# Convolution projection of a hybrid block: four groups of 1024 columns with the tokens on the result's partitions, in place of eight groups of 512 with the features there

## The chip, the cores and the metric

The kernel runs on one core of one Trainium2 chip. The metric is the device time of one execution in microseconds; of several runs the median is taken. A core has TensorE (PE: matmuls into PSUM), VectorE (DVE), ScalarE (ACT), GpSimd (POOL) and SyncE (SP, which issues most loads). Each engine works through its own queue in the order in which the program put it there, and engines wait for each other by semaphores.

## What is computed

One layer: the normalised input `h` (512 tokens, 2048 features) goes through one wide input projection, whose columns feed three branches. The change touches the first, a gated convolution of 1024 channels.

```python
proj = h @ w_in[l]
(c_gate, b_gate, u, conv_z, c_q, c_kv, k_rope_raw, mla_z,
 mem_q, mem_z, g_conv, g_mla, g_mem) = jnp.split(proj, split_at, axis=-1)
conv_y = b_gate * causal_depthwise_conv(c_gate * u, conv_w[l])
o_conv = (conv_y * jax.nn.silu(conv_z)) @ w_conv_out[l]
...
merged = (jax.nn.sigmoid(g_conv) * o_conv + jax.nn.sigmoid(g_mla) * o_mla
          + jax.nn.sigmoid(g_mem) * o_mem)
x = x + merged @ w_o[l]
```

The convolution has three taps over time (the token and the two before it), one set for each channel. `c_gate`, `b_gate`, `u` and `conv_z` have 1024 columns each, so 4096 columns of `w_in` belong to it.

## The kernel before

All is float32, and TensorE gets it in two parts, `hi` (the value as TensorE's fast float32 form holds it) and `lo` (what is left). A product is three matmuls, hi by hi, hi by lo and lo by hi (`mm3`, lines 153 to 155). Weights are split on the way: ACT writes `whi` (line 122), then DVE writes `wlo = raw - whi` (line 124). The pairs `whi`, `wlo` have three buffers, used in turn. Raw weights come in pieces of 128x1024 (512 KB) loaded by SP into ten buffers: four of `wpool` and six of `psw` (`take_raw`, `raws_free`).

The stages of the input projection use a scheme with seven block products in place of eight, on two by two blocks (`PRODUCTS`: P1, P7, P5, P6, P2, P4, P3). For it sums of weight blocks are made on DVE before they are split (`pre`), sums of activation blocks once (`x_forms`: `f` tiles and, by `place_t1`, the T1 blocks), and the seven results are put together from PSUM banks by DVE and ACT (`u`, `v`, `r`).

There are two forms of such a group. In `block_group` the weights are stationary and 256 tokens move: features lie on the result's partitions. A group has 512 columns, 14 chunks of 24 matmuls, 8 raw pieces loaded in pairs (line 943), and four PSUM banks of one tag. The convolution (`conv_group`, eight groups), `mla_z` (four) and the convolution's gate (four) use it. In `block_group_t` the activations are stationary and 512 weight columns move: tokens lie on the result's partitions. A group has 1024 columns, 28 chunks of 12 matmuls, 16 raw pieces loaded one by one (line 1054), and eight banks, four of each tag. The gates of the other two branches, the MLA output projection and the last projection use it.

A planner (`Chunk`, `drive`) writes the queues of PE, DVE, ACT and POOL. At every chunk it puts down, in this order: what is due by a hook (`at`), the weight sums of chunks up to three ahead (`pre`, `first`), the splits of chunks up to two ahead (`prep`, `lead`), what `phases` holds (matmuls of its own, such as transposes), pieces of other work as far as a budget of DVE time goes (`todo`, each with a cost and perhaps a chunk by which it must stand, `by`; then `spare`), and then the chunk's matmuls. A load is entered with `when_raw`: where no raw buffer is free it is put down again at the next chunk.

```python
def hook():
    if len(raws_free if kind is None else [k for k in raws_free if k == kind]) < n:
        when_raw(now[0] + 1, n, kind, fn)
    else:
        fn()
at[c].append(hook)
```

Of the convolution, `conv_group` takes a group's results with features on partitions and all 512 tokens in a row: it multiplies `c_gate` by `u` (line 1431), takes the taps (ACT line 1436, DVE line 1438 twice), multiplies by `b_gate` and by silu of `conv_z` (line 1443), and stores 128 channels to `adram` for the output projection, which comes much later. The stage ahead of it is `mem_z` (`plain_group`), the one behind it `mla_z`.

Of the kernel before, what the change touches and what calls it, by code (L numbers as in the profile page):

```python
# [94 lines left out]
def body(ctx, tc, a, out):  # L95
# [21 lines left out]
    def bank(tag):  # L117
        return psum.tile([P, 512], F32, tag=tag, name=tag)
# [95 lines left out]
    def g(col):  # L214
        return gains[:, col:col + 1]
# [824 lines left out]
                    k.done = results(name)  # L1040
        return first

    def block_group_t(src, tokens, results, early=6, opening=(), again=False):

        first = len(plan)
        w, kinds, bk, sc = {}, {}, {}, {}

        def load(i):
# [39 lines left out]

        for name, ch in order:
            bn, xn = {n: (b, x) for n, b, x in PRODUCTS}[name]
            hold = {}

            def pre(name=name, ch=ch, hold=hold):
                w00, w01 = w[ch], w[4 + ch]
                if name == "P7":
                    hold["s"] = psw.tile([P, KC, 512], F32, tag="s3", name="s3", bufs=2).rearrange("p k n -> p (k n)")
                    vec.tensor_tensor(out=hold["s"], in0=w00, in1=w01, op=ALU.subtract)  # L1100
                else:
                    hold["s"] = o = w01 if name == "P5" else w00
                    i0, i1, op = {"P5": lambda: (w01, w[8 + ch], ALU.add), "P6": lambda: (w01, w00, ALU.subtract),
                                  "P3": lambda: (w[12 + ch], w00, ALU.subtract)}[name]()
                    vec.tensor_tensor(out=o, in0=i0, in1=i1, op=op)  # L1105

            def prep(name=name, ch=ch, hold=hold):
                src_ = hold["s"] if "s" in hold else w[{"P1": 0, "P4": 8, "P2": 12}[name] + ch]
                hi, lo = parts_tile()
                split(src_, hi, lo)  # L1110
                raws_free.extend(kinds[i] for i in {"P5": (4 + ch,), "P4": (8 + ch,), "P3": (ch, 12 + ch)}.get(name, ()))
                hold["w"] = tuple(t.rearrange("p (k n) -> p k n", k=KC) for t in (hi, lo))

            def mm(name=name, ch=ch, bn=bn, xn=xn, hold=hold):
                opens = bn not in bk
                if not bk:

                    t, o = next_tag()
                    bk["tags"] = dict(zip("XWYZ", (t, t, o, o)))
                    if not again:  # L1120
                        tags[0] += 1
                if opens:
                    bk[bn] = [bank(bk["tags"][bn]) for _ in range(2)]
                last = name in ("P2", "P3", "P4", "P6")
                for tb in range(2):
                    cols = slice(tb * P, (tb + 1) * P)
# [19 lines left out]
    def f_tile(p):  # L1146
        return pf.tile([P, 2, 3, HS], F32R, name=f"f{p}")
# [205 lines left out]
    plan[first].lead = 1  # L1353
    take_memz(first, banks_z1, 1)

    tx = [None] * 8
    t1s = {}

    def x_forms(p):

# [14 lines left out]
                    nc.gpsimd.dma_start(out=eo[:, i], in_=hdram[k][:, 1], accum_op=ALU.add)  # L1375

        def sums():
            f = f_tile(p)
            tx[p] = operands(xt[p], xt[p + 8], f)
# [30 lines left out]
            at[CLOSE + 1 + p].append(lambda p=p: spare.extend(  # L1410
                (0.42, lambda q=q: place_t1(q)) for q in range(p - 3, p + 1)))

    for c, n in ((9, 12), (12, 4), (14, 0)):
        at[first + c].append(lambda n=n: flush_spare(n))


    def conv_group(cb):
        keep = {}

        def consume(half, r):  # L1420
            wc = G_CONV + 3 * cb
            if half:
                def silu():
                    keep["bz"] = r()
                    act.activation(r()[:, 1], r()[:, 1], AF.Silu)
                return [(1, 0, silu)]

            def cu():
                used["y"] += 1
                keep["cu"] = pres.tile([P, S], F32, tag="y", name="cu", bufs=4)  # L1430
                vec.tensor_tensor(out=keep["cu"], in0=r()[:, 0], in1=r()[:, 1], op=ALU.mult)

            def tap(n):
                cv, u = r()[:, 0, 2 - n:], keep["cu"][:, :S - 2 + n]
                if n == 2:
                    act.activation(cv, u, AF.Copy, scale=g(wc + 2))
                else:
                    vec.scalar_tensor_tensor(out=cv, in0=u, scalar=g(wc + n), in1=cv, op0=ALU.mult, op1=ALU.add)
                if n == 0:
                    freed("y")  # L1440

            def times(nb):
                vec.tensor_tensor(out=r()[:, 0], in0=r()[:, 0], in1=keep["bz"][:, nb], op=ALU.mult)
            return [(0, 0.69, cu), (1, 0, lambda: tap(2)), (1, 0.75, lambda: tap(1)), (1, 0.75, lambda: tap(0)),
                    (2, 0.69, lambda: times(0)), (2, 0.69, lambda: times(1)),
                    (4, 0, lambda: nc.scalar.dma_start(adram[8 + cb], r()[:, 0]))]
        return consume

    def mlaz_group(grp, first):
        ys = {}  # L1450
# [64 lines left out]
            return out_ + [(2, 0, lambda tb=tb: store(tb)) for tb in range(2)]  # L1515
        return results

    AFTER_PLAIN = (-3, -2, -1, 0)
    for cb in range(8):
        if cb == 0:  # L1520
            block_group(a["w_conv"][cb], tx, conv_group(cb), AFTER_PLAIN, halves=True)
        else:
            block_group(a["w_conv"][cb], tx, conv_group(cb))
    for grp in range(4):
        block_group(a["w_mlaz"][grp], tx, mlaz_group(grp, len(plan)))
    for grp in range(4):
# [308 lines left out]
def layout(inp):  # L1835
# [29 lines left out]
    a["w_conv"] = np.stack([two_by_two(w_in, [(c * 1024 + b * P, P) for c in (0, 2, 1, 3)]) for b in range(8)])  # L1865
# [22 lines left out]
```

## Time and profile before

| | us |
|---|---|
| median of 3 runs | 2144.67 |
| lowest and highest | 2143.73, 2145.27 |
| the profiled execution, its own time | 2144.14 |
| its span, first to last instruction | 2142.4 |
| PE busy | 2117.1 (99%) |
| DVE busy | 1565.1 (73%) |
| ACT busy | 1031.4 (48%) |
| mean granted TensorE clock | 0.999 |

The profile is of one execution. Busy time counts a moment once, however many matmuls overlap in it. A row of a timeline gives start, duration, engine, source line, tiles (out<-in) and, in brackets, how long the engine had been idle and who released it. Line numbers are those of the printed kernel.

### The profile page before, as it was taken

How to read it: one execution, taken by the hardware profiler on the slowest of the kernel's cores; microseconds unless marked ns; L12 is line 12 of the kernel's file. 1: busy time of each engine (PE TensorE's matmuls, PEld its weight loads, DVE VectorE, ACT ScalarE, POOL GpSimd, SP SyncE). 2: the span in 40 equal slices, each digit the busy share in tenths (PEclk: the TensorE clock that was granted, in tenths of full speed). 3: DMA queues.
4: the chain of work that ended last, by engine and by line, in shares of the span. 5: the costliest groups of instructions: out<-in, count | busy, mean ns of one | idle time of the engine just before them, and what ended most of it. 6: DMA issues, size and time to landing. Idle time of an engine off the chain costs nothing.

```text
span 2142.4 us, 31861 instructions
## 1 busy us (share of the span) xinstructions
PE 2117.1 (99%) x12504; PEld 1889.9 (88%) x12504; DVE 1565.1 (73%) x2230; ACT 1031.4 (48%) x1559; POOL 146.4 (7%) x193
## 2 busy tenths in 40 slices
PE   8999999999999999999999999999999999999999
PEld 6898888888888999999999999888888888887887
DVE  7853877773346877877877767777776788857987
ACT  7633676764334444444444444445445434434433
POOL 0000312120001000000000000000000001121000
PEclk9999999999999999999999999999999999999999
DMA  8572212144239324223345334344335755486452
GB/s 306 194 241 87 77 55 69 65 153 162 89 108 295 121 103 137 94 101 137 109 177 177 128 109 158 104 142 167 118 118 178 275 186 206 150 286 202 149 196 89
DMA packets 110119, 322.35 MB, mean 150 GB/s; under 512 B 13200, under 2 KB 13456, under 8 KB 109968
## 3 DMA queue, kind: packets, MB, share of 16 engines
q1 hardware_dynamic: 78480, 253.89, 34.3%
q10 hardware_dynamic: 21600, 38.63, 4.8%
q0 software_dynamic: 9888, 27.79, 4.7%
q8 instruction: 98, 1.61, 0.3%
q14 instruction: 53, 0.43, 0.1%
HBM read 269.41 MB, written 48.23 MB: 148 GB/s over the span
## 4 chain that ended last, share of the span: by engine, by line
PE 92%; DVE 3%; ACT 2%; DMA 1%; issue 1%; POOL 0%; ACTq 0%; DVEq 0%; POOLq 0%
PE acc L154 16%; PE acc L153 16%; PE acc L155 16%; PE aux L154 13%; PE aux L155 13%; PE aux L153 13%; PE aux L657 1%; PE aux L204 1%; DVE wlo L124 0%; ACT whi L146 0%; PE aux L637 0%; PE aux L638 0%; PE aux L639 0%; DMA mraw<-in_memT 0%; PE aux L641 0%
## 5 line engine op out<-in xcount | busy, mean ns | idle before, releaser
L122 ACT ACTIVATE whi<-raw 128x1024 fp32r<-128x1024 f32 x440 | 466.1, 1060 | 661.6 <-PE aux L154 159.1
L124 DVE TENSOR_TENSOR wlo<-raw,whi 128x1024 fp32r<-128x1024 f32 x440 | 538.6, 1225 | 336.1 <-ACT whi L122 329.0
L147 DVE TENSOR_TENSOR wlo<-raw,whi 128x1024 fp32r<-128x1024 f32 (+3 forms) x97 | 106.1, 1094 | 90.1 <-ACT whi L146 88.5
L146 ACT ACTIVATE whi<-raw 128x1024 fp32r<-128x1024 f32 (+3 forms) x97 | 92.8, 957 | 114.6 <-PE acc L154 41.6
L153 PE MATMUL acc<-whi,blk 128*128 128x512 f32 (+1 forms) x352 | 132.5, 380 | 2.1 <-DVE qt L582 1.4
L155 PE MATMUL acc<-whi,blk 128*128 128x512 f32 (+1 forms) x352 | 131.4, 374 | 0.0
L154 PE MATMUL acc<-wlo,blk 128*128 128x512 f32 (+1 forms) x352 | 131.1, 373 | 0.0
L1105 DVE TENSOR_TENSOR raw<-raw 128x1024 f32<-128x1024 f32 x96 | 116.9, 1218 | 0.0
L1015 DVE TENSOR_TENSOR raw<-raw 128x1024 f32<-128x1024 f32 x96 | 116.9, 1218 | 0.0
L122 ACT ACTIVATE whi<-s 128x1024 fp32r<-128x1024 f32 x64 | 67.9, 1061 | 93.6 <-PE aux L154 21.0
L155 PE MATMUL acc<-f,wlo 128*128 128x256 f32 x384 | 108.7, 283 | 0.0
L153 PE MATMUL acc<-f,whi 128*128 128x256 f32 x384 | 108.7, 283 | 0.0
L154 PE MATMUL acc<-f,whi 128*128 128x256 f32 x384 | 108.7, 283 | 0.0
L153 PE MATMUL aux<-f,whi 128*128 128x256 f32 x384 | 108.7, 283 | 0.0
L154 PE MATMUL aux<-f,whi 128*128 128x256 f32 x384 | 108.7, 283 | 0.0
L155 PE MATMUL aux<-f,wlo 128*128 128x256 f32 x384 | 108.7, 283 | 0.0
L1200 POOL DMA_DIRECT2D y<-gdram x48 | 26.4, 550 | 1198.2 <-DMA gdram<-gy 953.9
L154 PE MATMUL acc<-blk,whi 128*128 128x256 f32 (+1 forms) x320 | 97.5, 305 | 0.6 <-DVE blk L124 0.6
L153 PE MATMUL acc<-blk,whi 128*128 128x256 f32 (+1 forms) x320 | 97.8, 306 | 0.0
L153 PE MATMUL acc<-hU,whi 128*128 128x256 f32 (+1 forms) x320 | 97.5, 305 | 0.0
L153 PE MATMUL aux<-hU,whi 128*128 128x256 f32 (+1 forms) x320 | 97.5, 305 | 0.0
L153 PE MATMUL aux<-blk,whi 128*128 128x256 f32 (+1 forms) x320 | 97.4, 305 | 0.0
(458 smaller groups left out, 6239.4 us busy)
## 6 DMA issues: line engine op xcount, KB each, us to landing
raw<-in_w_conv SPq DMA_DIRECT2D x64, 512.0 KB, 4.3
raw<-in_w_mlaz SPq DMA_DIRECT2D x32, 512.0 KB, 5.0
raw<-in_w_gconv SPq DMA_DIRECT2D x32, 512.0 KB, 4.3
raw<-in_w_gmem SPq DMA_DIRECT2D x32, 512.0 KB, 3.3
raw<-in_w_gmla SPq DMA_DIRECT2D x32, 512.0 KB, 3.3
raw<-in_w_mla_out SPq DMA_DIRECT2D x32, 512.0 KB, 3.9
raw<-in_w_o SPq DMA_DIRECT2D x32, 512.0 KB, 3.7
raw<-in_w_mem_kv SPq DMA_DIRECT2D x31, 512.0 KB, 4.1
```

The costliest lines, as they stand in the source:

```text
L122: act.activation(hi, src, AF.Copy, scale=1.0 if g is None else g)
L124: vec.tensor_tensor(out=lo, in0=src, in1=r32(hi), op=ALU.subtract)
L146: act.activation(hi[:, cols], raw[:, cols], AF.Copy)
L147: vec.tensor_tensor(out=lo[:, cols], in0=raw[:, cols], in1=r32(hi[:, cols]), op=ALU.subtract)
L153: nc.tensor.matmul(o, lhsT=s[0], rhs=m[0], start=start, stop=False, skip_group_check=shared)
L154: nc.tensor.matmul(o, lhsT=s[0], rhs=m[1], start=False, stop=False, skip_group_check=shared)
L155: nc.tensor.matmul(o, lhsT=s[1], rhs=m[0], start=False, stop=stop, skip_group_check=shared)
L204: nc.tensor.transpose(out=b[:, i * P:(i + 1) * P], in_=s, identity=ident)
L657: nc.tensor.transpose(out=b[:, i * P:(i + 1) * P], in_=ps[i][:, j * P:(j + 1) * P], identity=ident)
L1015: vec.tensor_tensor(out=o, in0=i0, in1=i1, op=op)
L1105: vec.tensor_tensor(out=o, in0=i0, in1=i1, op=op)
L1200: eng.dma_start(t, src)
```

## The change

The convolution's projection becomes four groups of `block_group_t` (`conv_rows` in place of `conv_group`): a group holds 256 columns each of `c_gate`, `u`, `b_gate` and `conv_z`. The result of name "n t" (two by two blocks) now has tokens on the partitions: "0t" holds `c_gate` and `u` side by side, "1t" `b_gate` and `conv_z`. Their products are made there (`mul`, 256 wide), and then turned by 16 transposes of 128x128 for a group (`turn`, put down ahead of the fourth chunk of what follows), so that the taps run along the tokens as before. The group's order is that of `opening`: all chunks of P1 and P7, then those of P5 and P6, then P4, then P2 and P3. `paired` puts X and Y into banks of one tag and W and Z into the other, and turns the tags once for a group. The `f` tiles are now taken at one time (`x_operands`), and the last steps of the activations' forms are flushed one chunk later. The weights of the convolution are laid out in another order outside the kernel.

```diff
-    def block_group_t(src, tokens, results, early=6, opening=(), again=False):
+    def block_group_t(src, tokens, results, early=6, opening=(), again=False, paired=False):
...
             def mm(name=name, ch=ch, bn=bn, xn=xn, hold=hold):
-                opens = bn not in bk
+                opens = name in ("P1", "P7", "P5", "P6") and ch == 0
                 if not bk:
 
                     t, o = next_tag()
-                    bk["tags"] = dict(zip("XWYZ", (t, t, o, o)))
-                    if not again:
+                    bk["tags"] = dict(zip("XYWZ" if paired else "XWYZ", (t, t, o, o)))
+                    if not (again or paired):
                         tags[0] += 1
-                if opens:
-                    bk[bn] = [bank(bk["tags"][bn]) for _ in range(2)]
+                if opens and bn not in bk:
+                    for b in "WZ" if paired and bn == "Z" else bn:
+                        bk[b] = [bank(bk["tags"][b]) for _ in range(2)]
...
+    def x_operands():
+        for p in range(8):
+            fx[p] = f_tile(p)
+            tx[p] = operands(xt[p], xt[p + 8], fx[p])
+    at[CLOSE].append(x_operands)
...
-    for c, n in ((9, 12), (12, 4), (14, 0)):
+    for c, n in ((10, 12), (13, 4), (15, 0)):
         at[first + c].append(lambda n=n: flush_spare(n))
...
+        def turn():
+            t = keep["kind"]()
+            bs = [transpose4([s[:, f * P:(f + 1) * P] for s in b], t) for b in (cu, bz) for f in range(2)]
...
+                def tap(n, f=f, hold=hold, wc=wc):
+                    if n == 2:
+                        used["y"] += 1
+                        hold["t"] = pres.tile([P, S], F32, tag="y", name="cv", bufs=4)
+                        act.activation(hold["t"], bs[f], AF.Copy, scale=g(wc + 2))
+                        return
+                    cv = hold["t"][:, 2 - n:]
+                    vec.scalar_tensor_tensor(out=cv, in0=bs[f][:, :S - 2 + n], scalar=g(wc + n), in1=cv,
+                                             op0=ALU.mult, op1=ALU.add)
+
+                def times(f=f, hold=hold):
+                    vec.tensor_tensor(out=hold["t"], in0=hold["t"], in1=bs[2 + f], op=ALU.mult)
+                    later(1, 0, lambda: stored(f, hold["t"]))
...
+                later(0, 0, piece(lambda tap=tap: tap(2), **by))
+                later(0, 0.75, piece(lambda tap=tap: tap(1), **by))
+                later(0, 0.75, piece(lambda tap=tap: tap(0), **by))
+                later(0, 0.69, piece(times, **by))
+        phases[first + 31].append(turn)
...
-    for cb in range(8):
-        if cb == 0:
-            block_group(a["w_conv"][cb], tx, conv_group(cb), AFTER_PLAIN, halves=True)
-        else:
-            block_group(a["w_conv"][cb], tx, conv_group(cb))
+    for cb in range(4):
+        opening = [(n, ch) for n in ("P1", "P7") for ch in range(4)] if cb == 0 else \
+            [("P" + n, int(ch)) for n, ch in zip("11717177", "01021323")]
+        opening += [(n, ch) for ch in range(4) for n in ("P5", "P6")]
+        block_group_t(a["w_conv"][cb], tx, conv_rows(cb), 5 if cb == 0 else 6, opening, paired=True)
```

The new lines that the text below names are, in the changed kernel: L1057 the load of a piece, L1103 and L1108 the weight sums, L1435 `mul`, L1456 and L1476 the sums of results, L1472 the product taken from PSUM, L1504 the taps and L1508 the product by the gate. Names in the order that follows are tiles (out<-in); in brackets stand the semaphores that an instruction waits for, by the engine or the DMA queue that raises them.

PE, at the border between two groups of before (features on partitions, `hU` and `blk` moving):

```order
L153 MATMUL acc<-hU_6105,whi 128x256
L154 MATMUL acc<-hU_6105,whi 128x256
L155 MATMUL acc<-hU_6105,wlo 128x256
L153 MATMUL aux<-blk,whi 128x256 [waits Activation_49]
L154 MATMUL aux<-blk,whi 128x256
L155 MATMUL aux<-blk,wlo 128x256 [waits DVE_49]
```

PE, after the first three chunks of the second group of the changed kernel:

```order
L155 MATMUL aux<-whi,f_7176 128x512
L204 MATMUL acc<-ident,cu 128x128
L204 MATMUL acc<-ident,cu 128x128 [waits DVE_49]
L204 MATMUL acc<-ident,u_7691 128x128 [waits DVE_49] x2
L204 MATMUL acc<-ident,cu 128x128 x2
L204 MATMUL acc<-ident,u_7691 128x128 x2
L204 MATMUL acc<-ident,v_7790 128x128 [waits PE_49]
L204 MATMUL acc<-ident,v_7790 128x128 x3
```

The matmuls have gone from 256 to 512 columns, and the transposes of the group before, which wait for DVE, stand among those of the next.

DVE, in a group of before, from the product of `c_gate` and `u` to the first sum of the next results:

```order
L1431 TENSOR_TENSOR cu<-r_8390 128x512
L1015 TENSOR_TENSOR raw<-raw 128x1024
L124 TENSOR_TENSOR wlo<-raw,whi 128x1024 [waits DVE_49,PE_49,Activation_49]
L1015 TENSOR_TENSOR raw<-raw 128x1024
L124 TENSOR_TENSOR wlo<-raw,whi 128x1024 [waits PE_49,Activation_49]
L1438 SCALAR_TENSOR_TENSOR r_8390<-cu,gains,r_8390 128x511
L1438 SCALAR_TENSOR_TENSOR r_8390<-cu,gains,r_8390 128x510 [waits DVE_49]
L124 TENSOR_TENSOR wlo<-raw,whi 128x1024 [waits PE_49,Activation_49]
L1443 TENSOR_TENSOR r_8390<-r_8390,r_8330 128x512 [waits DVE_49] x2
L124 TENSOR_TENSOR wlo<-raw,whi 128x1024 [waits DMAHW6_49,PE_49,Activation_49]
```

DVE, in the second group of the changed kernel, from the first tap to the `wlo` of chunk 11 (the chunks P5 and P6 of the first two quarters):

```order
L1504 SCALAR_TENSOR_TENSOR cv<-acc,gains,cv 128x511
L1504 SCALAR_TENSOR_TENSOR cv<-acc,gains,cv 128x510 [waits DVE_49]
L1508 TENSOR_TENSOR cv<-cv,acc 128x512 [waits DVE_49]
L1108 TENSOR_TENSOR raw<-raw 128x1024
L124 TENSOR_TENSOR wlo<-raw,whi 128x1024 [waits Activation_49]
L1108 TENSOR_TENSOR raw<-raw 128x1024 [waits DMAHW0_49]
L124 TENSOR_TENSOR wlo<-raw,whi 128x1024 [waits Activation_49]
L1108 TENSOR_TENSOR raw<-raw 128x1024 [waits DVE_49]
L124 TENSOR_TENSOR wlo<-raw,whi 128x1024 [waits Activation_49]
L1108 TENSOR_TENSOR raw<-raw 128x1024 [waits DMAHW4_49]
L124 TENSOR_TENSOR wlo<-raw,whi 128x1024 [waits Activation_49]
```

The same taps of two blocks stand in one piece ahead of the first P5's split (the first block's three are just ahead of these rows), and a sum that waits for a load (DMAHW4) stands ahead of a split that needs none.

SP, the loads of the second group of the changed kernel from its piece 8 on:

```order
L1057 DMA raw<-in_w_conv 128x1024 [waits DMAHW7_49,DVE_49]
L1057 DMA raw<-in_w_conv 128x1024 [waits DMAHW0_49]
L1057 DMA raw<-in_w_conv 128x1024 [waits DMAHW1_49,DVE_49]
L1057 DMA raw<-in_w_conv 128x1024 [waits DMAHW4_49,DVE_49]
L1057 DMA raw<-in_w_conv 128x1024 [waits DMAHW5_49,DVE_49]
```

A load raises the semaphore of the queue that it names first: these are the pieces 8, 9, 11, 10 and 12 in this order, and the third and fourth wait for DVE to have read a buffer.

## Rows read from the trace of the kernel before

**Rows 1.** The page: its head, part 1 (busy time and share of the span of each engine) and the first line of part 4 (the chain of work that ended last, by engine).

```profile
span 2142.4 us, 31861 instructions
...
PE 2117.1 (99%) x12504; PEld 1889.9 (88%) x12504; DVE 1565.1 (73%) x2230; ACT 1031.4 (48%) x1559; POOL 146.4 (7%) x193
...
PE 92%; DVE 3%; ACT 2%; DMA 1%; issue 1%; POOL 0%; ACTq 0%; DVEq 0%; POOLq 0%
```

**Rows 2.** Windows: the first convolution group, the second, and a group of `block_group_t` (a gate); columns are the stretch, its length, busy time and instructions of PE, PE's weight loads, DVE, ACT and POOL, granted clock, DMA share and GB/s.

```profile
694.29:735.45 41.16, 40.57 (x337) 40.36 (x336) 33.18 (x40) 20.69 (x28) 0.00 (x0) 1.00 0.40 142
735.45:775.77 40.32, 40.32 (x338) 40.32 (x337) 32.20 (x33) 17.55 (x19) 0.00 (x0) 1.00 0.32 112
...
1340.00:1416.10 76.10, 76.10 (x339) 63.06 (x338) 57.32 (x53) 35.94 (x40) 0.00 (x0) 1.00 0.40 139
```

**Rows 3.** Timeline of PE: the first matmul of the convolution, the one gap in its first group, and the first matmul of the stage behind it.

```profile
694.29 0.28 PE L153 MATMUL acc<-blk,whi 128*128 128x256 f32 x1
...
711.93 0.29 PE L153 MATMUL acc<-blk,whi 128*128 128x256 f32 x1
712.82 0.38 PE L154 MATMUL acc<-blk,whi 128*128 128x256 f32 x1 [0.59 <-DVE blk L124]
...
1017.70 0.28 PE L153 MATMUL acc<-blk,whi 128*128 128x256 f32 x1
```

**Rows 4.** Timeline of PE in the stage `mem_z`, 512 moving: two matmuls with 143 others between them, back to back.

```profile
639.89 0.39 PE L153 MATMUL acc<-hU,whi 128*128 128x512 f32 x1
...
672.53 0.39 PE L153 MATMUL aux<-hU,whi 128*128 128x512 f32 x1
```

**Rows 5.** Timeline of PE at a block of 16 transposes in the convolution's output projection.

```profile
1902.67 0.39 PE L155 MATMUL acc<-act,wlo 128*128 128x512 f32 x1
1902.90 1.91 PE L1701 MATMUL aux<-ident,f 128*128 128x128 f32 x16
1904.56 0.48 PE L153 MATMUL acc<-act,whi 128*128 128x512 f32 x1
1904.88 0.40 PE L154 MATMUL acc<-act,whi 128*128 128x512 f32 x1
```

**Rows 6.** Groups of DVE instructions by line and shape (count, busy us, mean ns of one), in the convolution's groups two to eight and, the last, around its first group.

```profile
L124 DVE TENSOR_TENSOR wlo<-raw,whi 128x1024 fp32r<-128x1024 f32 x84 | 102.7, 1223 | 52.4 <-ACT whi L122 51.5
L1015 DVE TENSOR_TENSOR raw<-raw 128x1024 f32<-128x1024 f32 x42 | 51.1, 1218 | 0.0
...
L1443 DVE TENSOR_TENSOR r<-r,r 128x512 f32<-128x512 f32 x14 | 9.6, 689 | 0.2
...
L1154 DVE TENSOR_TENSOR raw<-eo 128x256 f32<-128x256 f32 x7 | 2.9, 418 | 0.0
```

**Rows 7.** Timeline of DVE in the third convolution group around the taps: a weight sum, a split, the two taps, a split and two products.

```profile
787.47 1.22 DVE L1015 TENSOR_TENSOR raw<-raw 128x1024 f32<-128x1024 f32 x1
788.61 1.22 DVE L124 TENSOR_TENSOR wlo<-raw,whi 128x1024 fp32r<-128x1024 f32 x1
789.74 1.53 DVE L1438 SCALAR_TENSOR_TENSOR r<-cu,gains,r 128x511 f32<-128x511 f32 x2
791.40 1.23 DVE L124 TENSOR_TENSOR wlo<-raw,whi 128x1024 fp32r<-128x1024 f32 x1
792.55 1.41 DVE L1443 TENSOR_TENSOR r<-r,r 128x512 f32<-128x512 f32 x2
794.28 1.23 DVE L124 TENSOR_TENSOR wlo<-raw,whi 128x1024 fp32r<-128x1024 f32 x1 [0.32 <-ACT whi L122]
```

**Rows 8.** Timelines of PE, ACT and DVE in a group of `block_group_t`: the last matmul of a chunk, the `whi` that waits for it, and the `wlo` behind that.

```profile
1418.94 0.39 PE L155 MATMUL aux<-whi,blk 128*128 128x512 f32 x1
...
1419.42 1.06 ACT L122 ACTIVATE whi<-raw 128x1024 fp32r<-128x1024 f32 x1 [1.66 <-PE aux L155]
...
1420.51 1.23 DVE L124 TENSOR_TENSOR wlo<-raw,whi 128x1024 fp32r<-128x1024 f32 x1 [0.30 <-ACT whi L122]
```

**Rows 9.** Timelines of DVE and of SP's queue: a `wlo` that gives back its raw buffer, and the load that goes into it.

```profile
1406.86 1.23 DVE L124 TENSOR_TENSOR wlo<-raw,whi 128x1024 fp32r<-128x1024 f32 x1 [0.36 <-ACT whi L122]
...
1408.12 0.33 SPq L1054 DMA_DIRECT2D raw<-in_w_gmem  x1
```

**Rows 10.** DMA issues, each with its count, KB and median us from issue to landing: of 1393 to 1394 (a lone load), of 1394 to 1395 (a load issued 1.4 us behind that one), of 1418.9 to 1420.2 (a load with two stores), and of the whole span for the convolution's weights.

```profile
raw<-in_w_gmem SPq DMA_DIRECT2D x1, 512.0 KB, 3.2
...
raw<-in_w_gmem SPq DMA_DIRECT2D x1, 512.0 KB, 4.1
...
raw<-in_w_gmem SPq DMA_DIRECT2D x1, 512.0 KB, 4.2
gdram<-gy ACTq DMA_DIRECT2D x2, 256.0 KB, 4.6
...
raw<-in_w_conv SPq DMA_DIRECT2D x64, 512.0 KB, 4.3
```

**Rows 11.** Timeline of PE around the one fall of the granted clock in mid-kernel.

```profile
1962.96 0.71 PE L1701 MATMUL acc<-ident,f 128*128 128x128 f32 x5
1966.24 1.26 PE L1701 MATMUL acc<-ident,f 128*128 128x128 f32 x8 [2.57 <-ACT hU L1715]
1967.16 0.78 PE L153 MATMUL aux<-act,whi 128*128 128x512 f32 x1
...
1970.29 0.52 PE L154 MATMUL aux<-act,whi 128*128 128x512 f32 x1
1970.65 0.39 PE L155 MATMUL aux<-act,wlo 128*128 128x512 f32 x1
...
1967.00:1971.00 4.00, 4.00 (x14) 3.25 (x13) 3.87 (x8) 2.59 (x5) 1.09 (x2) 0.57 0.59 197
```

More of the change, by code (lines that the diff above doesn't have):

```diff
@@ L1041, in block_group @@
         return first
-    def block_group_t(src, tokens, results, early=6, opening=(), again=False):
+    def block_group_t(src, tokens, results, early=6, opening=(), again=False, paired=False):
         first = len(plan)
         w, kinds, bk, sc = {}, {}, {}, {}
+        if paired:
+            results.keep["kind"] = lambda: bk["tags"]["X"]
         def load(i):
@@ L1354, in body @@
     take_memz(first, banks_z1, 1)
-    tx = [None] * 8
+    tx, fx = [None] * 8, [None] * 8
     t1s = {}
+    def x_operands():
[3 more added lines that the diff above has]
+    at[CLOSE].append(x_operands)
     def x_forms(p):
@@ L1377, in sums @@
         def sums():
-            f = f_tile(p)
-            tx[p] = operands(xt[p], xt[p + 8], f)
+            f = fx[p]
             if p % 4 == 0:
@@ L1411, in body @@
                 (0.42, lambda q=q: place_t1(q)) for q in range(p - 3, p + 1)))
-    for c, n in ((9, 12), (12, 4), (14, 0)):
+    for c, n in ((10, 12), (13, 4), (15, 0)):
         at[first + c].append(lambda n=n: flush_spare(n))
[L1417 to L1436, printed above, removed]
-                else:
-                    vec.scalar_tensor_tensor(out=cv, in0=u, scalar=g(wc + n), in1=cv, op0=ALU.mult, op1=ALU.add)
-                if n == 0:
-                    freed("y")
[L1442 to L1447, printed above, removed]
@@ new lines, in conv_rows, with mul, results, silu @@
+    def conv_rows(cb):
+        first = len(plan)
+        cu, bz, keep = [None] * NTB, [None] * NTB, {}
+        hcols, lcols = slice(HS, 2 * HS), slice(0, HS)
+        def mul(o, t):
+            vec.tensor_tensor(out=o, in0=t[:, lcols], in1=t[:, hcols], op=ALU.mult)
+        def results(name, o, i0, i1):
+            out_ = []
+            last = dict(by=first + 30)
+            for tb in range(2):
+                if name == "11":
+                    def silu(tb=tb):
+                        act.activation(o(tb)[:, hcols], o(tb)[:, hcols], AF.Silu)
+                    def gate(tb=tb):
+                        keep[tb] = o(tb)
+                        bz[2 + tb] = o(tb)[:, lcols]
+                        mul(bz[2 + tb], o(tb))
+                    out_ += [(0, 0, piece(silu, **last)), (1, 0.42, piece(gate, **last))]
+                elif name == "10":
+                    hold = {}
+                    def sums(tb=tb, hold=hold):
+                        used["y"] += 1
+                        hold["t"] = pres.tile([P, S], F32, tag="y", name="gy", bufs=4)
+                        vec.tensor_tensor(out=hold["t"], in0=i0(tb), in1=i1(tb), op=ALU.add)
+                        act.activation(hold["t"][:, hcols], hold["t"][:, hcols], AF.Silu)
+                    def gate(tb=tb, hold=hold):
+                        bz[tb] = keep[tb][:, hcols]
+                        mul(bz[tb], hold["t"])
+                        freed("y")
+                    out_ += [(0, 0.69, piece(sums, by=first + 24)), (1, 0.42, piece(gate, **last))]
+                elif name == "00":
+                    def both(tb=tb):
+                        if tb == 0:
+                            used["y"] += 1
+                            keep["cu"] = pres.tile([P, S], F32, tag="y", name="cu", bufs=4)
+                        cu[tb] = keep["cu"][:, tb * HS:(tb + 1) * HS]
+                        act.activation(cu[tb], i0(tb)[:, hcols], AF.Copy)
+                        vec.tensor_tensor(out=cu[tb], in0=i0(tb)[:, lcols], in1=cu[tb], op=ALU.mult)
+                    out_ += [(0, 0.42, piece(both, **last))]
+                else:
+                    def sums(tb=tb):
+                        vec.tensor_tensor(out=o(tb), in0=i0(tb), in1=i1(tb), op=ALU.add)
+                    def both(tb=tb):
+                        cu[2 + tb] = o(tb)[:, lcols]
+                        mul(cu[2 + tb], o(tb))
+                    out_ += [(0, 0.69, piece(sums, by=first + 28)), (0, 0.42, piece(both, **last))]
+            if name == "01":
+                out_.sort(key=lambda t: -t[1])
+            return out_
+        def turn():
+            t = keep["kind"]()
+            bs = [transpose4([s[:, f * P:(f + 1) * P] for s in b], t) for b in (cu, bz) for f in range(2)]
+            freed("y")
+            freed("r0")
+            freed("r1")
+            by = dict(by=first + 33)
+            for f in range(2):
+                hold = {}
+                wc = G_CONV + 3 * (2 * cb + f)
+                def tap(n, f=f, hold=hold, wc=wc):
+                    if n == 2:
+                        used["y"] += 1
+                        hold["t"] = pres.tile([P, S], F32, tag="y", name="cv", bufs=4)
[7 more added lines that the diff above has]
+                    later(1, 0, lambda: stored(f, hold["t"]))
+                def stored(f, t):
+                    nc.scalar.dma_start(adram[8 + 2 * cb + f], t)
+                    freed("y")
+                later(0, 0, piece(lambda tap=tap: tap(2), **by))
[3 more added lines that the diff above has]
+        phases[first + 31].append(turn)
+        results.keep = keep
+        return results
@@ L1516, in gate_rows @@
         return results
-    AFTER_PLAIN = (-3, -2, -1, 0)
-    for cb in range(8):
-        if cb == 0:
-            block_group(a["w_conv"][cb], tx, conv_group(cb), AFTER_PLAIN, halves=True)
-        else:
-            block_group(a["w_conv"][cb], tx, conv_group(cb))
+    for cb in range(4):
[3 more added lines that the diff above has]
+        block_group_t(a["w_conv"][cb], tx, conv_rows(cb), 5 if cb == 0 else 6, opening, paired=True)
     for grp in range(4):
@@ L1864, in layout @@
     a["w_mem_out"] = groups(i["w_mem_out"][0], 0, 2048)
-    a["w_conv"] = np.stack([two_by_two(w_in, [(c * 1024 + b * P, P) for c in (0, 2, 1, 3)]) for b in range(8)])
+    a["w_conv"] = np.stack([two_by_two_t(np.concatenate([w_in[:, c * 1024 + b * HS:c * 1024 + (b + 1) * HS] for c in (0, 2, 1, 3)], axis=1))
+                            for b in range(4)])
     a["w_gconv"] = np.stack([two_by_two(w_in, [(9280 + i * 512, 512)]) for i in range(4)])
```

## The prediction

> **What bounds the kernel now.** Read the page first: TensorE is busy for 99% of a span of 2142.4 us and the chain that ended last is 92% PE, while DVE is at 73% and ACT at 48% [rows 1]. So the time is nearly the sum of matmul pitches (start of one to start of the next), plus the moments when PE waits. The duration in a row of a matmul (0.28 us, 0.39 us) is no price, because matmuls overlap; the pitch has to be taken from two starts far apart.
>
> Next the windows table. A convolution group of before takes 40.32 us on PE, and DVE is busy for 32.2 us of it, ACT for 17.6; the first group takes 41.16 [rows 2]. The stage runs from 694.29 to 1017.70, 323.41 us for 2688 matmuls with 256 moving [rows 3]. One gap is in it: the matmul after 711.93 starts at 712.82 and not 0.12 later, for lack of a `wlo` from DVE [rows 3]. Less that 0.8, the pitch is 322.6 / 2688 = 0.120 us.
>
> **Part 1, the matmuls.** The change does the same seven products with 4 x 336 = 1344 matmuls, 512 moving. Such a matmul stands in the trace already: from 639.89 to 672.53 are 144 of them, 0.2267 us each [rows 4]. 1344 x 0.2267 = 304.7 us, against 323.4: **-18.7 us**. PE is the bound here, so all of it counts. The Trainium skill ("TensorE: Matmul & The Clock Gate", section "Back-to-back issue gap") gives columns / 2.4 plus 2.5 ns for an isolated gap, 109 and 216 ns; by that the trade would give 3.5 us and not 17.9. The rows decide: both pitches are 11 ns longer, and that fixed part is paid half as often.
>
> **Part 2, the transposes.** Each group ends in `turn`: 16 transposes of 128x128 from SBUF. The trace has 16 such in a row: they start at 1902.90, the matmul behind them at 1904.56 and the next at 1904.88; from 1902.67 to 1904.88 is 2.21 us, of which two matmuls are 0.45, so 1.76 for the block [rows 5]. 4 x 1.76 = **+7.0 us**, all on PE. The Trainium skill (same page, "Part 4: PE-mode transpose") gives about 275 ns for one. The rows agree on the duration, not on the cost in a row: 64 x 275 ns would be 17.6 us, where the pitch gives 7.0.
>
> **Part 3, DVE and the waits that it makes.** DVE works in strict order, so I lay its queue end to end with row prices: `wlo` and a weight sum 1.14 us from start to start, a tap 0.83 (the second waits for the first), a 512-wide product 0.6, a 256-wide one 0.33 [rows 6, 7]. A split starts late, not early: ACT may write `whi` only when the buffer used three chunks before is read; it starts 0.25 us after the next chunk's first matmul (1419.42 against 1419.17, which is 1418.94 + 0.23), and DVE's `wlo` starts 1.34 after it [rows 8]. A chunk is 12 x 0.2267 = 2.72 us.
>
> *The turn.* It stands ahead of chunk 3 of the next group, at 3 x 2.72 = 8.16 us. Its last operands (L1435, two products) stand behind the `wlo` of chunk 4, which starts at 5.44 + 1.34 = 6.78; + 1.14 + 0.33 + 0.42 = 8.67. PE wants the fourth transpose at 8.47: 0.2 us, three times, and about twice that in front of the next stage: **+1.0 us**.
>
> *The taps.* Four taps and two products are queued ahead of the `wlo` of chunk 8, the first P5. Counted from the start of chunk 5: 1.34, `wlo` of chunk 7 1.14, taps and products 2 x (1.66 + 0.6) = 4.5, a weight sum 1.13, `wlo` of chunk 8 1.22: 9.33. PE wants it at 8.16 + 0.23 = 8.39: 0.9 us, in three groups: **+2.7 us**. In groups of before two taps stand there and DVE still had idle time left [rows 2, 7].
>
> *The loads.* This is the term that decides. The group now holds 16 raw pieces in 10 buffers. Pieces 0 to 7 stay until P5 and P3, 8 and 9 take the last two; 10 and 11 must wait for buffers that the `wlo` of P5 gives back. `when_raw` puts off a load that finds no buffer by re-entering it behind those due later, so piece 11 goes first although piece 10 is used first (the order shows the two waits the other way round). Piece 10 is then issued only after the `wlo` of chunk 10. The sum for P5 of chunk 12 needs it, and the `wlo` of chunk 11 is queued behind that sum. From the same zero: `wlo` of chunk 8 starts at 8.11; sum, `wlo`, sum take 1.14 + 3 x 1.13 until `wlo` of chunk 10 starts at 12.64, ending at 13.86. A freed buffer's load is issued 0.03 us later (1406.86 + 1.23 = 1408.09, issue 1408.12) [rows 9]. Landing: 3.2 us for a lone load, 4.2 beside two stores issued with it, 4.1 when it follows another by 1.4 us, 4.3 the median of this matrix's loads in pairs [rows 10]. ACT issues the group's two stores at this very place, so I take 4.1: 18.0; sum 1.13, `wlo` 1.22: 20.35. PE wants it at 8.16 + 0.94 + 3 x 2.72 + 0.23 = 17.49. **2.9 us, three times: +8.6** (bounds 2.0 and 3.1 each, for 3.2 and 4.3).
>
> In group 0 no taps stand, but the rest of the activations' forms do. Piece 9 takes the buffer of the T1 scratch, free after the last `blk` split. From PE's first matmul: 1.15, then 7 `wlo` and 6 sums 14.8, four 512-wide gates 2.5, nine 256-wide pieces 3.1, a split 0.6, short waits 0.7: 22.8. Landing behind piece 10's load 4.0, sum 1.13, `wlo` 1.22: 29.2, wanted at 9 x 2.72 + 0.23 = 24.7: **+4.5 us** (3.7 to 4.8).
>
> **Part 4, the clock.** The granted clock fell once in the middle of before: five transposes from 1962.96, 2.57 us idle, eight more, and from 1967.16 matmuls come 0.43 us apart, the 1.2 GHz level, until about 1970.65 [rows 11]. Eight matmuls took 3.5 us and not 1.8: 1.7 us lost. Ahead of it the engine had had 4.2 us of only transposes and idle time. Group 0's wait of 4.5 is longer, so I count **one fall, +1.7**; the 2.9 us waits are between nothing and this, and I count none for them (bound: three, +5.1).
>
> What costs nothing: the bytes loaded are the same; ACT has 22 us free of 40 [rows 2]; the form steps moved one chunk later have P1's and P7's eight chunks ahead of T1's first use; the `adram` stores are read hundreds of us later.
>
> **Sum.** -18.7 + 7.0 + 1.0 + 2.7 + 8.6 + 4.5 + 1.7 = +6.8. The profiled execution took 2144.14 us, its span and 1.7 around it, 0.5 under the median of 2144.67 and within its runs: 2144.1 + 6.8 = **2150.9**, said as 2151.
>
> **Rivals.** *The loads land like lone ones* (3.2 us, rows 10): the waits shrink by 0.8 + 3 x 0.9 = 3.5, and with no fall of the clock the time is 2145.7, no change to be seen. For it: loads are now single. Against: stores and a second load stand beside each of the four. Chance 0.22.
>
> *The loads do not hold DVE at all*, the other side: a buffer free one chunk and a half earlier than I lay it, so that piece 10 lands before DVE comes to its sum (it decides below about 1.2 us from the end of chunk 10's `wlo`, or if piece 10 goes first). Then only the small waits stay: 2144.1 - 18.7 + 7.0 + 1.0 + 2.7 = 2136.1. For it: before shows no PE wait for any load of this matrix. Against: there the loads went in pairs with eight pieces to a group. Chance 0.08.
>
> *All at its worst*: loads of 5.3 us as two crowded ones would give, and a fall of the clock after every wait: 2150.9 + 4.8 + 5.1 = 2160.8. Chance 0.07.
>
> *No gain in a wider matmul*, 512 moving at twice 0.120: 1344 x 0.240 = 322.6, 2168.8. The Trainium skill's gap rule of part 1 leans this way. Rows 4 speak against it. Chance 0.01.
>
> **How the numbers follow.** The forecast has 0.62, from 2149.2 (no fall) to 2156.0 (four). A measurement can tell about 0.2% of this kernel, 4.3 us, from no change, so slower begins at 2149.0: 0.62 + 0.07 + 0.01, less 0.05 for the forecast's own lower edge, 0.65. Same: 0.22 + 0.05 = 0.27. Faster: 0.08. The range takes in the first rival and the falls of the clock, 2145 to 2157, and leaves out the other rivals and the edges.
>
> **What would show it.** Right: conv matmuls 0.227 apart; blocks of 16 transposes of 1.76; in each later group a PE wait of about 3 us for `wlo` in chunk 11, with DVE idle for a DMA ahead of L1108; about 4.5 us in chunk 9 of group 0. Wrong: no DVE wait for `raw<-in_w_conv`, PE without gaps over 1 us, or a stage (first convolution matmul to the first of `mla_z`, transposes included) under 318 us.

## The result and the profile after

The changed kernel takes 2150.91 us (median of 7 runs, 2149.8 to 2154.13), the kernel before 2144.64 (7 runs, 2141.26 to 2145.27): a ratio of 1.0034, 95% interval 1.0023 to 1.0046. It is slower, by little more than a measurement can tell. The profiled execution took 2151.38, its span 2149.6, at a mean granted clock of 0.997.

The page of the changed kernel first, its head, part 1, the two lines of part 4 and one group of part 5.

```profile
span 2149.6 us, 29212 instructions
...
PE 2113.2 (98%) x11224; PEld 1828.5 (85%) x11224; DVE 1566.0 (73%) x2246; ACT 1030.8 (48%) x1567; POOL 146.3 (7%) x193
...
PE 89%; DVE 5%; ACT 3%; DMA 2%; issue 1%; SPq 0%; POOL 0%; ACTq 0%; DVEq 0%; POOLq 0%
PE acc L154 16%; PE acc L153 15%; PE acc L155 15%; PE aux L154 13%; PE aux L155 13%; PE aux L153 13%; DVE wlo L124 1%; DVE raw L1108 1%; PE aux L204 1%; DMA raw<-in_w_conv 1%; PE aux L657 1%; ACT whi L122 0%; DMA raw<-in_w_conv_out 0%; DVE cv L1504 0%; PE aux L637 0%
...
L1108 DVE TENSOR_TENSOR raw<-raw 128x1024 f32<-128x1024 f32 x144 | 175.4, 1218 | 15.0 <-DMA raw<-in_w_conv 15.0
```

Against [rows 1], 1280 matmuls are gone and the busy time of PE fell by only 3.9 us; PE's share of the chain fell from 92% to 89%, and DVE, ACT and DMA took it over. The last line is the new thing: DVE stood idle for 15.0 us ahead of weight sums, for loads of the convolution's weights. The view of waits says who paid (engine, line, waited for, total us, times, longest).

```profile
PE aux L154 <- DVE wlo L124: 8.1, 4, 4.6
...
PE acc L154 <- DVE wlo L124: 5.2, 4, 1.9
```

and, for DVE:

```profile
DVE raw L1108 <- DMA raw<-in_w_conv: 15.0, 4, 4.4
```

Four waits of DVE for a load, one in each group. The timeline of PE shows where they come out: first and last matmul of the stage (the last row belongs to `mla_z`), the gap in chunk 9 of group 0, two matmuls of a quiet stretch, one block of transposes, and chunks 8 and 11 of group 1.

```profile
695.96 0.39 PE L153 MATMUL acc<-whi,blk 128*128 128x512 f32 x1
...
720.60 0.39 PE L153 MATMUL aux<-whi,f 128*128 128x512 f32 x1
725.60 0.80 PE L154 MATMUL aux<-wlo,f 128*128 128x512 f32 x1 [4.61 <-DVE wlo L124]
...
739.71 0.39 PE L155 MATMUL aux<-whi,f 128*128 128x512 f32 x1
...
759.89 0.39 PE L154 MATMUL aux<-wlo,hU 128*128 128x512 f32 x1
...
786.63 0.39 PE L155 MATMUL aux<-whi,f 128*128 128x512 f32 x1
786.87 0.38 PE L204 MATMUL acc<-ident,cu 128*128 128x128 f32 x2
...
788.03 1.04 PE L204 MATMUL acc<-ident,v 128*128 128x128 f32 x8
788.83 0.47 PE L153 MATMUL aux<-whi,blk 128*128 128x512 f32 x1
789.14 0.39 PE L154 MATMUL aux<-wlo,blk 128*128 128x512 f32 x1
...
802.55 0.39 PE L153 MATMUL acc<-whi,blk 128*128 128x512 f32 x1
803.62 0.50 PE L154 MATMUL acc<-wlo,blk 128*128 128x512 f32 x1 [0.68 <-DVE wlo L124]
...
811.69 0.39 PE L153 MATMUL acc<-whi,f 128*128 128x512 f32 x1
814.02 0.67 PE L154 MATMUL acc<-wlo,f 128*128 128x512 f32 x1 [1.94 <-DVE wlo L124]
...
1024.84 0.28 PE L153 MATMUL acc<-blk,whi 128*128 128x256 f32 x1
```

A gap costs its start-to-start distance less one pitch. Group 0 loses 5.00 - 0.23 = 4.77 us, chunk 8 loses 0.84, chunk 11 2.10; groups 2 and 3 read the same way, 0.84 and 0.84, 2.25 and 2.06. From 739.71 to 759.89 are 89 pitches of 0.2267. The stage takes 328.88 us, against 323.41 before [rows 3], and one block of transposes still lies behind it.

The cause of the wait in chunk 11 of group 1 can be read from three timelines (DVE, SP's queue, ACT's queue). They are put in order of time within each engine.

```profile
806.89 1.22 DVE L124 TENSOR_TENSOR wlo<-raw,whi 128x1024 fp32r<-128x1024 f32 x1
811.61 1.23 DVE L1108 TENSOR_TENSOR raw<-raw 128x1024 f32<-128x1024 f32 x1 [3.50 <-DMA raw<-in_w_conv]
812.75 1.22 DVE L124 TENSOR_TENSOR wlo<-raw,whi 128x1024 fp32r<-128x1024 f32 x1
...
808.14 0.33 SPq L1057 DMA_DIRECT2D raw<-in_w_conv  x1
...
807.10 0.81 ACTq L1512 DMA_DIRECT2D adram<-cv  x2
```

The `wlo` of chunk 10 ends at 808.11 and gives back a buffer; 0.03 later piece 10 is issued into it. The sum that needs piece 10 starts at 811.61, and the `wlo` of chunk 11, which needs no load, stands behind that sum and starts at 812.75; 1.27 later PE goes on.

Windows of the two falls of the clock in the stage and of a third, in the attention stage (same columns as [rows 2]):

```profile
725.44:728.85 3.41, 3.25 (x8) 2.57 (x9) 3.41 (x4) 2.17 (x4) 0.00 (x0) 0.50 0.03 2
814.18:817.60 3.42, 3.42 (x9) 2.68 (x10) 3.42 (x4) 1.06 (x1) 0.00 (x0) 0.50 0.14 11
264.64:268.05 3.41, 3.41 (x13) 3.19 (x13) 1.45 (x8) 1.75 (x6) 0.00 (x0) 0.50 0.22 80
```

In each the granted clock is 0.50, 1.2 of 2.4 GHz. The first sets in 0.16 us before a wait of PE ends (725.60), the second 0.16 us after one (814.02); the eight pitches from 725.60 end at 729.04 and took 3.44 us in place of 1.81, so a fall costs 1.6 us.

### The profile page after: what moved, and what is told of

It reads as the page before. It is cut to its first block, busy times and chain, and to the rows that moved or that the text cites. A ratio compares the mean times of both kernels' runs of the same rounds, so it can differ in the third digit from the quotient of the medians.

```text
span 2149.6 us, 29212 instructions
## 1 busy us (share of the span) xinstructions
PE 2113.2 (98%) x11224; PEld 1828.5 (85%) x11224; DVE 1566.0 (73%) x2246; ACT 1030.8 (48%) x1567; POOL 146.3 (7%) x193
## 4 chain that ended last, share of the span: by engine, by line
PE 89%; DVE 5%; ACT 3%; DMA 2%; issue 1%; SPq 0%; POOL 0%; ACTq 0%; DVEq 0%; POOLq 0%
PE acc L154 16%; PE acc L153 15%; PE acc L155 15%; PE aux L154 13%; PE aux L155 13%; PE aux L153 13%; DVE wlo L124 1%; DVE raw L1108 1%; PE aux L204 1%; DMA raw<-in_w_conv 1%; PE aux L657 1%; ACT whi L122 0%; DMA raw<-in_w_conv_out 0%; DVE cv L1504 0%; PE aux L637 0%
## 5 line engine op out<-in xcount | busy, mean ns | idle before, releaser
L1108 DVE TENSOR_TENSOR raw<-raw 128x1024 f32<-128x1024 f32 x144 | 175.4, 1218 | 15.0 <-DMA raw<-in_w_conv 15.0
L154 PE MATMUL aux<-wlo,f 128*128 128x512 f32 x288 | 113.3, 393 | 7.4 <-DVE wlo L124 7.4
L154 PE MATMUL acc<-wlo,f 128*128 128x512 f32 x288 | 113.0, 392 | 3.8 <-DVE wlo L124 3.8
L153 PE MATMUL acc<-whi,f 128*128 128x512 f32 x288 | 112.7, 391 | 0.4 <-DVE y L1661 0.4
L155 PE MATMUL acc<-whi,f 128*128 128x512 f32 x288 | 112.8, 392 | 0.0
L155 PE MATMUL aux<-whi,f 128*128 128x512 f32 x288 | 112.6, 391 | 0.0
L153 PE MATMUL aux<-whi,f 128*128 128x512 f32 x288 | 112.5, 391 | 0.0
L124 DVE TENSOR_TENSOR wlo<-s,whi 128x1024 fp32r<-128x1024 f32 x64 | 78.3, 1223 | 23.7 <-ACT whi L122 23.6
L153 PEld LDWEIGHTS acc<-whi,blk 128*128 128x128 f32 x416 | 78.1, 188 | 15.4 <-ACT kn L560 2.2
L154 PEld LDWEIGHTS acc<-wlo,blk 128*128 128x128 f32 x416 | 78.3, 188 | 12.9 <-DVE wlo L124 2.2
L154 PE MATMUL aux<-wlo,blk 128*128 128x512 f32 x224 | 87.4, 390 | 0.8 <-DVE wlo L124 0.7
L155 PEld LDWEIGHTS acc<-whi,blk 128*128 128x128 f32 x416 | 78.1, 188 | 11.2
L155 PE MATMUL aux<-whi,blk 128*128 128x512 f32 x224 | 87.0, 389 | 0.0
```

Of the source, the lines that this page charges most:

```text
L124: vec.tensor_tensor(out=lo, in0=src, in1=r32(hi), op=ALU.subtract)
L153: nc.tensor.matmul(o, lhsT=s[0], rhs=m[0], start=start, stop=False, skip_group_check=shared)
L154: nc.tensor.matmul(o, lhsT=s[0], rhs=m[1], start=False, stop=False, skip_group_check=shared)
L155: nc.tensor.matmul(o, lhsT=s[1], rhs=m[0], start=False, stop=stop, skip_group_check=shared)
```

## The experiments

The theory (A in the expectations): DVE's strict order and the order of the re-entered loads make the waits, because piece 11 takes the first free buffer and piece 10, needed first, the next. The rivals: DVE has simply too much queued there, loads or not (B); the loads land late for the sake of the DMA queues alone; the matmul trade or the transposes were priced wrongly. Each experiment is compared with runs of the kernel before beside it, whose median was 2142.24 in the first three and in that of the matmuls of half the width, and 2143.03 in the other three.

**Loads in order of use.**

```diff
+        asked = []
...
-                when_raw(max(-3, first + d), 1, None, lambda i=4 * b + ch: load(i))
+                asked.append(4 * b + ch)
+                when_raw(max(-3, first + d), 1, None,
+                         (lambda: load(asked.pop(0))) if paired else (lambda i=4 * b + ch: load(i)))
```

> Only the order of the loads differs: a re-entered load of a group takes the next piece in order of use, so piece 10 goes ahead of piece 11. Theory A (order of the loads): the waits of 2.1 to 2.3 us for `wlo` in chunk 11 of groups 1 to 3 vanish, the 4.8 us wait in chunk 9 of group 0 shrinks to about 3; 8 us less, and up to 3.4 more if the clock falls that followed these waits go too: 2139 to 2143 us, faster than before by 0.1 to 0.25%. Theory B (DVE simply has too much queued there, loads or not): the waits stay or move to chunk 12, under 1.5 us gained: 2149.5 to 2151.

Measured: 2138.17 us, ratio 0.9983 (0.9975 to 0.9992). The waits of PE and of DVE in this run:

```profile
PE aux L154 <- DVE wlo L124: 3.7, 3, 2.5
...
PE acc L154 <- DVE wlo L124: 1.4, 2, 0.7
```

```profile
DVE raw L1111 <- DMA raw<-in_w_conv: 3.1, 2, 2.3
```

The three waits in chunk 11 are gone (through it matmuls come 0.227 apart), group 0's fell from 4.77 to 2.69, and the waits of 0.84 in chunk 8 stay. No fall of the clock is left in the stage, which takes 316.9 us in place of 328.9. This is as A has it. The median lies under the 2139 to 2143 of A, but the kernel before beside it was faster too; by the ratio, 0.17% faster, it is within what A said. B is out for chunk 11: PE, DVE and ACT run the same instructions in the same order as in the changed kernel, and PE no longer waits there (DVE itself still waits once in the later groups, 0.7 us, for a load).

**The product later.** The product by the gate is due later, in its fourth chunk from the turn on; Z and W exchange the order in which they take their banks, so that the transposed blocks may stay in theirs for longer.

```diff
-                    for b in "WZ" if paired and bn == "Z" else bn:
+                    for b in "ZW" if paired and bn == "Z" else bn:
...
-                later(0, 0.69, piece(times, **by))
+                later(0, 0.69, piece(times, by=first + 34))
```

> The product by the gate (L1508, four per group, 0.6 us each) is due one chunk later than the taps, so that DVE reaches the split of chunk 8 sooner; the loads stay as in the changed kernel. Theory A: the wait of 0.84 us in chunk 8 falls to about 0.2, and the one in chunk 11 grows to about 2.6, since DVE has a fixed amount of work before piece 10's sum and now less cover: 2150 us, within 1 us of the changed kernel. Theory B (each wait is a price by itself): 2 us less, 2148.5 to 2149.

Measured: 2151.53 us, ratio 1.005 (1.0037 to 1.0064). PE in chunk 11 of group 1:

```profile
812.30 0.50 PE L154 MATMUL acc<-wlo,f 128*128 128x512 f32 x1 [2.38 <-DVE wlo L124]
```

No gap in chunk 8 is over 0.3 us any more, and chunk 11 waits 2.54 (2.77 less a pitch) in place of 2.10, 2.64 and 2.68 in the later groups. The time didn't fall. As A says, the two waits are not two prices: whoever passes the first sooner waits longer at the second, which hangs on the load. Together the waits of the two chunks were 8.9 us in the changed kernel and are 8.3 here. There were three falls of the clock in the stage, one more than in the profile of the changed kernel; the ratios of the two to the kernel before have intervals that overlap.

**Loads, product and forms together.** Both edits above, and the last steps of the activations' forms flushed earlier, so that group 0's buffer comes free sooner.

```diff
-    for c, n in ((10, 12), (13, 4), (15, 0)):
+    for c, n in ((10, 12), (12, 4), (13, 0)):
```

> Loads in order of use, the product one chunk later, and the last steps of the activations' forms flushed up to two chunks earlier than in the changed kernel. Theory A: no wait above 1 us is left in groups 1 to 3, group 0's is about 1 to 1.5; 2134 to 2138 us, 0.3 to 0.5% faster than before. Theory B: 2147 to 2150.

Measured: 2134.56 us, ratio 0.9966 (0.9954 to 0.9979), faster than both kernels. Its waits of PE for `wlo`:

```profile
PE aux L154 <- DVE wlo L124: 1.3, 3, 0.6
...
PE acc L154 <- DVE wlo L124: 0.9, 2, 0.6
```

Of the 13.3 us that PE waited in these two lines of the changed kernel 2.2 are left. So the change of form was worth having; what made it slower were waits that the order of loads, and of two small pieces of DVE work, put there.

**Loads and forms, without the later product.**

> Loads in order of use and the forms flushed earlier, the product left with the taps. Tells apart what each of the two small edits of best_order_forms gave: group 0's wait falls from 2.9 to about 1.3 in two pieces, the three waits of 0.84 in chunk 8 stay; 2135.5 to 2137.5 us, between e1_order and best_order_forms. Rival (the flush alone is what counts): within 0.5 us of 2134.6.

Measured: 2136.24 us, ratio 0.9969 (0.9957 to 0.9981). Its waits of PE for `wlo`:

```profile
PE acc L154 <- DVE wlo L124: 2.2, 4, 0.7
PE aux L154 <- DVE wlo L124: 1.2, 2, 0.7
```

The trace is as expected: group 0's wait is in two pieces (0.43 and 0.76), the three of 0.84 in chunk 8 stay. The span is 1.9 us longer than with the later product. By the medians the two differ by 1.7 us, against the kernel before beside each by 0.9, and their intervals overlap. So the times don't settle whether the flush alone counts; only the traces tell these apart.

**Matmuls of half the width.** The changed kernel, with each 512-wide convolution matmul in two.

```diff
-                        mm3(bk[bn][tb], (x[0][:, cols], x[1][:, cols]), tuple(t[:, k] for t in hold["w"]),
-                            opens and k == 0, ch == 3 and k == KC - 1, True)
+                        for q in ((slice(0, HS), slice(HS, S)) if paired else (slice(0, S),)):
+                            mm3(bk[bn][tb][:, q], (x[0][:, cols], x[1][:, cols]), tuple(t[:, k, q] for t in hold["w"]),
+                                opens and k == 0 and q.start == 0, ch == 3 and k == KC - 1, True)
```

> The changed kernel with each convolution matmul of 512 moving cut into two of 256, 2688 again; everything else stays. Pitch theory (0.120 us for 256, 0.2267 for 512, so 11 ns fixed a matmul more than columns by 2.4 GHz): 17.9 us more matmul time, some 4 us of it taken back because the waits of chunk 11 and group 0 shrink under longer chunks: 2163 to 2166. Rival (a fixed part of 2.5 ns a matmul): 3.5 us more, less the same kind of cover: 2151 to 2154.

Measured: 2163.08 us, ratio 1.0096 (1.0083 to 1.011). PE at the stage's start and end, and two matmuls of a quiet stretch:

```profile
694.74 0.28 PE L153 MATMUL acc<-whi,blk 128*128 128x256 f32 x1
...
739.84 0.28 PE L153 MATMUL aux<-whi,f 128*128 128x256 f32 x1
...
760.00 0.28 PE L153 MATMUL acc<-whi,hU 128*128 128x256 f32 x1
...
1035.12 0.28 PE L153 MATMUL acc<-blk,whi 128*128 128x256 f32 x1
```

168 pitches in 20.16 us are 0.120 each. The stage is 340.38 us, 11.5 longer. Under longer chunks the waits shrank, by 1.07 in group 0, 3 x 0.37 in chunk 8 and 1.35 in chunk 11, and one fall of 1.6 is missing: 11.5 + 1.07 + 1.1 + 1.35 + 1.6 = 16.6 of the 17.9 that the pitches give; of the other 1.3 the three blocks of transposes make 0.5 (1.89 each in place of 2.05), and the rest I haven't traced. The two pitches differ by 226.7 - 120.0 = 106.7 ns for 256 columns, which is 2.4 GHz, so 13.3 ns is left as the fixed part at either width, not 11 as the expectation has it. The rival's 3.5 is out. The Trainium skill ("TensorE: Matmul & The Clock Gate", section "Back-to-back issue gap") would have given about that by its gap for an isolated matmul (1344 x 2.5 ns, 3.4 us, as an estimate); here the measurement decides, and it is near 17.

**Transposes left out.** The version with all three edits, with the tile `cu` read where the transposed blocks were.

```diff
-            bs = [transpose4([s[:, f * P:(f + 1) * P] for s in b], t) for b in (cu, bz) for f in range(2)]
+            bs = [keep["cu"]] * 4
```

> The version of best_order_forms with its 64 transposes left out (taps and products read the tile `cu` in their place; that part of the computation is missing). With hardly a wait left in that version the difference is what the transposes cost on PE. By the pitch of the rows (1.76 a block of 16, some 0.2 more at each for the change of shape and short waits for DVE): 7 to 8.3 us less, 2126 to 2127.5. Rival, each transposition at its full duration of about 275 ns: 17.6 less, 2117.

Measured: 2126.64 us, ratio 0.9919 (0.9906 to 0.9931), 7.9 below the version that has them (8.7 when each is taken against the kernel before beside it). The stage's first matmul and the first of `mla_z`, with the transposes:

```profile
694.30 0.39 PE L153 MATMUL acc<-whi,blk 128*128 128x512 f32 x1
...
1007.52 0.28 PE L153 MATMUL acc<-blk,whi 128*128 128x256 f32 x1
```

and without:

```profile
693.63 0.39 PE L153 MATMUL acc<-whi,blk 128*128 128x512 f32 x1
...
1000.59 0.28 PE L153 MATMUL acc<-blk,whi 128*128 128x256 f32 x1
```

313.22 against 306.96 us, with three blocks in the stage: 2.09 each, 8.3 for four. The rival's 17.6 is out.

**Taps left out.** The second and third tap, on DVE, are not done.

```diff
                     cv = hold["t"][:, 2 - n:]
-                    vec.scalar_tensor_tensor(out=cv, in0=bs[f][:, :S - 2 + n], scalar=g(wc + n), in1=cv,
-                                             op0=ALU.mult, op1=ALU.add)
+                    return
```

> The changed kernel without the two DVE taps of each block (16 instructions of some 0.8 us; that part of the computation is missing), loads in the changed kernel's order. Theory A says the wait in chunk 11 is the late load of piece 10 plus whatever DVE has queued ahead of the buffer that it waits for: 3.3 us less queued there, so the waits of chunk 8 vanish and those of chunk 11 fall from 2.1 to about 0.3, group 0's 4.8 stays: some 8 us less, with a clock fall fewer 10: 2141 to 2143. Rival (the load lands late for reasons of the DMA queues alone): the chunk 11 waits stay near 2, 2148.

Measured: 2144.34 us, ratio 1.0004 (0.9995 to 1.0013). The waits in chunk 8 are gone, group 0's stays at 4.71, and those in chunk 11 fell to 0.96, 1.05 and 0.87, not to 0.3: between the two theories, as the time is, above A's 2141 to 2143 and below the rival's 2148. In order, the waits of PE for `wlo`, the end of the split of chunk 10 in group 1, SP's issue of piece 10, and DVE's sum that waits for it:

```profile
PE aux L154 <- DVE wlo L124: 6.0, 3, 4.6
PE acc L154 <- DVE wlo L124: 1.5, 2, 0.8
...
803.29 1.23 DVE L124 TENSOR_TENSOR wlo<-raw,whi 128x1024 fp32r<-128x1024 f32 x1
...
804.54 0.33 SPq L1057 DMA_DIRECT2D raw<-in_w_conv  x1
...
808.89 1.23 DVE L1108 TENSOR_TENSOR raw<-raw 128x1024 f32<-128x1024 f32 x1 [4.37 <-DMA raw<-in_w_conv]
```

DMA issues from 804 to 812 (count, KB, median us to landing):

```profile
raw<-in_w_conv SPq DMA_DIRECT2D x1, 512.0 KB, 4.3
adram<-cv ACTq DMA_DIRECT2D x2, 256.0 KB, 4.7
```

The load was still issued 0.02 us after the `wlo` of chunk 10 ended (803.29 + 1.23), so the chain is that of A, but it landed in 4.3 us, not in the 3.6 that I had worked with. That is the 0.7 by which the wait missed A's 0.3. DVE's taps ahead and the landing both set the wait.

## Why the prediction was right, step by step

The forecast of 2150.9 came out at 2150.91, by the likeliest case. The size is partly luck, because two terms were off in opposite directions.

| term | said | measured |
|---|---|---|
| matmuls | -18.7 | -18.7 by the pitch of 0.2267; halving them gave back 16.6 of 17.9 |
| transposes and turn | +7.0 and +1.0 | 4 x 2.06 = +8.2 (786.63 to 789.14 less two pitches) |
| taps, chunk 8 | +2.7 | 3 x 0.84 = +2.5 |
| loads, chunk 11 | +8.6 | 2.10 + 2.25 + 2.06 = +6.4 |
| group 0, chunk 9 | +4.5 | +4.8 |
| clock, in the stage | +1.7 | two falls of 1.6, +3.2 |
| sum | +6.8 | +6.4 |

The medians differ by 6.3; the two profiled executions, from which the table is read, by 7.2, and so do their spans. Of the other 0.8, the pitch behind a wait, 0.33 or 0.34 where no fall stands, makes 0.11 five times, 0.55. The stage starts 1.67 later for the fall in the attention stage; behind it the span has the same 1124.7 us as before although a block of transposes has been added there, since the fall near 1967 [rows 11] did not come again and a wait there is shorter. A start 1.67 later and 2.06 less behind it make -0.4 together, and aren't the change's. So about 0.6 of the 7.2 isn't traced.

One row price was read too low: a 512-wide product at 0.6 us, where [rows 7] gives 0.72 from start to start (1.41 less the 0.69 of one). In the changed kernel it is 0.61 (798.44 to 799.05), so the term of the taps came out near all the same.

*The mechanism of the loads* was as laid out: piece 10 issued 0.03 us after the `wlo` of chunk 10, the sum waiting, a split that needs no load waiting behind it. The order of the loads alone, put right, took the three waits away. *Its size* was 0.7 too large each: I took 4.1 us for the landing from [rows 10], where stores go out with the load, and it took 3.4, 3.6 and 3.4 in the three groups (in group 1 from 808.14 until the sum could start). The stores had been issued a microsecond earlier (807.10). The DMA issues of the changed kernel from 807 to 812:

```profile
adram<-cv ACTq DMA_DIRECT2D x2, 256.0 KB, 2.2
raw<-in_w_conv SPq DMA_DIRECT2D x1, 512.0 KB, 3.4
```

In group 0 the landing took 4.4 us where I had 4.0, and the term is 0.3 larger.

*The clock.* I counted a fall for group 0 and none for the shorter waits, with three as the bound. One of the three came, behind 1.94 us of idle time. That term was too small by 1.5, while the loads were too large by 2.2. The comparison behind it was also misread: the first row of [rows 11] begins inside a block of eight transposes. Whole, it is

```profile
1962.63 1.04 PE L1701 MATMUL acc<-ident,f 128*128 128x128 f32 x8
```

so the stretch of transposes and idle time ahead of that fall was 4.5 us, not 4.2, and group 0's wait, priced at 4.5, was no longer than it.

*The rivals.* "The loads do not hold DVE at all" was priced at 2136.1. The changed kernel isn't that case, but the experiment with piece 10 first is, but for the 2.7 us that still wait in group 0. The rival's 8.0 below before, less 2.7, makes 5.3; measured were 4.1 below the kernel before beside it. "Loads land like lone ones" came half true, 3.4 to 3.6 us in the later groups and yet 4.4 in group 0. In the later groups its wait of 2.0 was nearer than the forecast's 2.9; what kept the total at the forecast is group 0 and two falls of the clock, where this rival has none. The signs named for the forecast are there: the pitch, the two places of waiting, DVE idle ahead of L1108, and a stage far above 318 us; only the waits in chunk 11 are 2.1 and not 3, and a block of transposes costs 2.06 and not 1.76. The wider matmul gains what the rows said.

## What to carry to other kernels

When a group holds more pieces than there are buffers, look at the order in which put-off loads come back: one that overtakes an earlier piece stops an engine with a strict order, and with it work that needs no load. Price a wider matmul by the pitch of two starts far apart, and transposes in a row by the pitch as well. A wait that hangs on a load isn't shortened by giving the engine ahead of it less to do, unless that also issues the load sooner.

## What was not expected of the hardware

Which waits are followed by a fall of the clock can't be told from their length alone. In the profiles of this study idle times of PE of 4.61, 4.55, 4.30 and 3.54 us in the convolution's groups all went with one; of 2.53 (loads in order of use), 2.52 and 2.10 us did not, of 2.48, 2.38 and 1.94 did; of 1.90 and less none did. What decides between 1.9 and 2.6 us stays open. It also moves from run to run: the mean clock of the seven runs of the changed kernel is 0.996 to 0.998, and the two at 0.996 are the longest, 2153.75 and 2154.13.

Two stores of 256 KB and a load of 512 KB make each other late or not depending on who comes first. With the stores issued 1.0 us ahead of the load (changed kernel, three groups) the load landed in 3.4 to 3.6 us and the stores in 2.0 to 2.5; with the stores 0.4 us behind it (taps left out, three groups) it took 4.2 to 4.4, and the stores 4.5 to 4.9.
